# Score rows in at most two pieces, the last one negated in place with a chained minimum

## The chip, the cores and the metric

The kernel runs on one core of a Trainium2 chip. The metric is the device time of one execution in microseconds. The core has five engines with queues of their own: PE (matrix products; PEld is its weight load), DVE (VectorE), ACT (ScalarE), POOL (GpSimd) and SP, which issues the transfers. They meet only at semaphores, and each of them runs its instructions in the order in which the program lists them.

## What is computed

A decoder layer on 2048 tokens of width 1024: a normalisation, one input projection, two groups of heads, one output projection, a normalisation and the residual. The change touches differential attention alone: 8 heads, each with two score maps over 64 channels, rows of 128 queries.

```python
def diff_attention(q, k, v, lam):
    for i in range(S // Q_BLOCK):                 # 16 blocks of 128 queries
        q0 = i * Q_BLOCK
        end = q0 + Q_BLOCK
        s = jnp.einsum('bqhcd,bkhcd->bhcqk', q[:, q0:end], k[:, :end]) * scale
        ...
        p = jax.nn.softmax(jnp.where(causal, s, -jnp.inf), axis=-1)
        w = p[:, :, 0] - lam * p[:, :, 1]
        outs.append(jnp.einsum('bhqk,bkhe->bqhe', w, v[:, :end]))
```

## The kernel before

The program has five stretches: projections for the first half of the tokens (0 to about 600 us), attention of that half (to about 1090 us, called half A here), projections and the recurrence of the second half (to about 1370 us), attention of the second half (to about 2080 us, half B), and the rest of the output projection. Matrix products that have nothing to do with attention are mixed into both attention stretches as fill: projections of the second half into A (L227), the output projection into B (tile `f`, L1073).

**Units.** Attention works through units (head h, pair of query blocks pr, block t, map c). A unit is 128 rows of n x 128 score columns, n = 2 pr + t + 1. In half A n runs from 1 to 8, in half B from 9 to 16; each half has 8 heads x 16 units = 128 units. Below, "unit 14/0" is the one with n = 14 and c = 0, and "pair 14" are its two maps, 14/0 and 14/1.

**A unit's life.** Its columns are cut into pieces of SP = 512, one PSUM tile `s` each: 3 or 4 in half B. `score_mm` (L441) writes a piece with two products per 512 columns. `score_max` reduces it on DVE: all pieces but the last by a maximum into a column of `mx` (L457), the last by an addition of the causal mask that also gives the maximum (L460, with a read of the accumulator behind it); a fourth kind of instruction takes the maximum over the columns and negates it (L464, tile `nm`). `score_exp` (L480) then runs one exponential per piece on ACT, from `s` to `p`, with `nm` as bias. When both maps of a block are done, `combine` adds up the sums (L489, `lch`), makes two factors (L493, L494, `rr`) and forms p0 + factor x p1 over the whole row (L498). The result is transposed in groups of four 128x128 blocks into `pw` (L512), split into two parts by ACT (`wh`, L516) and DVE (`wl`, L517), and multiplied with the values into `o` (L535). Every second pair index a norm follows (L547 to L580).

**PSUM.** Half B has eight banks of 512 columns of f32: four tiles `s` of one bank, two `pw`, one `o`, one `f`. A piece of the next unit can be written only when the exponential of the unit that held the tile has read it. With three pieces a unit leaves one tile free; with four it leaves none.

**What sets the order.** `attention` writes, unit by unit, the exponentials of the present unit and then, by a small planner with a clock (`tp`, `free`), the next unit's score pieces between transposes, fill and value products; `combine` and the norm stand at the unit's end. The program that the tile framework makes of it lists instructions in another order where its own scheduling finds them ready at other times, so the order on each engine is read from the built program and not from the source.

Of the kernel before, what the change touches and what calls it, by code (L numbers as in the profile page):

```python
# [8 lines left out]
F32 = mybir.dt.float32  # L9
F32R = mybir.dt.float32r  # L10
BF16 = mybir.dt.bfloat16
# [17 lines left out]
MASKED = -1.0e38  # L29
SP = 512  # L30
NSA = 3
# [12 lines left out]
def hymba_kernel(  # L44
# [56 lines left out]
    make_identity(nc, ident)  # L101
    mask16 = const.tile([P, CH], BF16, name="mask16")
    nc.vector.memset(mask16, 0.0)
    ones2 = const.tile([P, 2], F32, name="ones2")
# [20 lines left out]
    def setup():  # L125
        rows, lq = su["rows"], su["lq"]
        with tc.tile_pool(name="setup", bufs=1) as sp, tc.tile_pool(name="setup_ps", bufs=1, space=PSUM) as spp:
# [4 lines left out]
            )  # L132
            nc.vector.tensor_copy(out=mask16[:, CH - P:], in_=m32)
            pt = spp.tile([P, 80], F32, name="pt")
# [255 lines left out]

    def attention(prs, kv_p, pools, nsb, per_slot, kbufs, vbufs, p1bufs):

# [34 lines left out]
        def pieces(u):  # L427
            n = (2 * u[1] + u[2] + 1) * P
            return n, [(c0, min(n, c0 + SP)) for c0 in range(0, n, SP)]

# [15 lines left out]

        def score_max(u, pi):
            n, pcs = pieces(u)
            c0, c1 = pcs[pi]
            if pi == 0:  # L450
                negm[u] = e_p.tile([P, 1], F32, tag="nm", name="nm", bufs=4)
            if pi == 0:
                sc[u, "mx"] = e_p.tile([P, 4], F32, tag="mx", name="mx", bufs=4)
            mx = sc[u, "mx"]
            s = sc[u, pi][:, 0:c1 - c0]
            if pi < len(pcs) - 1:
                nc.vector.tensor_reduce(out=mx[:, pi:pi + 1], in_=s, axis=AX.X, op=ALU.max)  # L457
                return

            nc.vector.tensor_tensor_reduce(  # L460
                out=s, in0=s, in1=mask16[:, CH - (c1 - c0):], scale=1.0, scalar=MASKED, op0=ALU.add, op1=ALU.max,
                accum_out=mx[:, pi:pi + 1],
            )
            nc.vector.tensor_reduce(out=negm[u], in_=mx[:, 0:pi + 1], axis=AX.X, op=ALU.max, negate=True)  # L464

        def score_exp(u):
# [8 lines left out]
            for pi, (c0, c1) in enumerate(pcs):  # L475
                if len(pcs) == 1:
                    acc = lch[h, pr // 2][:, (2 * pr + t) % 4, c:c + 1]
                else:
                    acc = sc[u[:3]][:, c, pi:pi + 1]
                nc.scalar.activation(  # L480
                    out=p[:, c0:c1], in_=sc.pop((u, pi))[:, 0:c1 - c0], func=AF.Exp, bias=negm[u], accum_out=acc,
                )
# [141 lines left out]
        yield  # L624
        e_p, a_p, ps_s, ps_w, ps_o, fill = pools
        for h, j in early:
            load_v(h, j)
# [4 lines left out]
        for s in range(U + 12):  # L632
# [13 lines left out]
            if u:  # L646
                score_exp(u)
            tp = 0.15 + SP / 1200.0
            free = [0.0 if k < nsb - na else tp * (k - nsb + 1 + na) + 0.1 for k in range(npc)]
# [41 lines left out]
    def attention_of(half):  # L691

        st = ExitStack()
        kv_p = st.enter_context(tc.tile_pool(name="kv" + half, bufs=2, side="right"))
        pools = []
        if half == "A":
            gen = attention(range(0, 4), kv_p, pools, NSA, lambda s: FA, 4, 4, 2)
        else:
            gen = attention(range(4, 8), kv_p, pools, 4 * CH // SP, lambda s: FB if s > 1 else 6, 6, 5, 1)
        next(gen)  # L700
        return st, pools, gen
# [333 lines left out]
    with ExitStack() as pb:  # L1035
# [3 lines left out]
        a_p = pb.enter_context(tc.tile_pool(name="attB", bufs=2, side="right"))  # L1039
        ps_s = pb.enter_context(tc.tile_pool(name="ps_sB", bufs=4 * CH // SP, space=PSUM))  # L1040
        ps_w = pb.enter_context(tc.tile_pool(name="ps_wB", bufs=2, space=PSUM))
# [156 lines left out]
```

## Time and profile before

| | |
|---|---|
| runs of the kernel | 2242.29, 2247.93, 2249.29 us, median 2247.93 |
| the profiled execution | 2245.1 us, of which the span of the trace is 2243.2 us and 1.9 us lie around it |
| PE busy | 2149.8 us (96%) |
| DVE busy | 1505.0 us (67%) |
| ACT busy | 1003.3 us (45%) |
| POOL busy | 803.1 us (36%) |
| granted PE clock over the span | 0.987 |

Matrix products are pipelined: the next one starts before the last one has ended, so a PE that is busy all the time can still be slower than its own spacing. A page's group line gives the line of the code, the engine, the tiles, the number of instructions, their busy time, the mean of one, and the idle time in front of them with what ended it.

### The profile page before, as it was taken

The numbers are of one execution on the slowest core, as the hardware profiler recorded it, in microseconds if no ns is written. First come the engines' busy times: TensorE is split into PE (matmuls) and PEld (weight loads), VectorE is DVE, ScalarE is ACT, GpSimd is POOL, SyncE is SP. The second block draws the span as 40 slices with busy tenths as digits, with TensorE's granted clock in tenths as the row PEclk, the third lists the DMA queues.
The fourth block names the chain that finished last, engine by engine and source line by source line (L and its number), as shares of the span: only waits on it lengthen the run. The fifth ranks groups of instructions, "written<-read, shape, count | busy, mean of one in ns | idle before, by whom it ended". The sixth has DMA issues, their size and how long they took to land. (4 is left out here: it accounts for less than half of the span.)

```text
span 2243.2 us, 31726 instructions
## 1 busy us (share of the span) xinstructions
PE 2149.8 (96%) x11025; PEld 1786.9 (80%) x11025; DVE 1505.0 (67%) x3296; ACT 1003.3 (45%) x2259; POOL 803.1 (36%) x741
## 2 busy tenths in 40 slices
PE   7999999999899999999999998999999999999888
PEld 7888888888688888788888776888888887888666
DVE  6531144556677767777437776888888888889775
ACT  4211133444544444444225655665656656566211
POOL 1223044434411111111265653233533335345542
PEclk9999999999999999999999998999999999999999
DMA  6554332332478666665452207455464465654573
GB/s 214 151 155 150 103 102 78 97 104 77 117 195 218 165 172 169 175 168 133 132 182 70 67 33 178 117 150 143 124 177 127 124 168 140 169 160 142 161 230 131
DMA packets 346497, 317.93 MB, mean 142 GB/s; under 512 B 20257, under 2 KB 278370, under 8 KB 346338
## 3 DMA queue, kind: packets, MB, share of 16 engines
q1 hardware_dynamic: 346338, 315.91, 50.5%
q8 instruction: 87, 1.43, 0.3%
q14 instruction: 72, 0.59, 0.1%
HBM read 221.41 MB, written 94.44 MB: 141 GB/s over the span
## 5 line engine op out<-in xcount | busy, mean ns | idle before, releaser
L227 PE MATMUL ps<-hh,whi 128*128 128x512 f32 (+1 forms) x1456 | 563.7, 387 | 0.0
L227 PE MATMUL ps<-hh,wlo 128*128 128x512 f32 (+1 forms) x1456 | 562.9, 387 | 0.0
L227 PE MATMUL ps<-hl,whi 128*128 128x512 f32 (+1 forms) x1456 | 561.5, 386 | 0.0
L480 ACT ACTIVATE p<-s,nm 128x512 f32<-128x512 f32 (+3 forms) x640 | 392.6, 623 | 325.4 <-DVE nm L464 284.3
L199 POOL TENSOR_TENSOR wlo<-wraw,whi 128x1024 fp32r<-128x1024 f32 x88 | 221.8, 2521 | 526.4 <-DVE whi L198 173.4
L441 PE MATMUL s<-ks,qs 128*128 128x512 f32 (+2 forms) x1280 | 370.5, 387 | 19.3 <-ACT p L480 15.5
L227 PEld LDWEIGHTS ps<-hl,whi 128*128 128x128 f32 x1456 | 275.3, 189 | 51.7
L457 DVE TENSOR_REDUCE mx<-s 128x1 f32<-128x512 f32 x384 | 257.8, 684 | 87.4 <-PE s L441 86.1
L227 PEld LDWEIGHTS ps<-hh,wlo 128*128 128x128 f32 x1456 | 275.2, 189 | 51.5
L227 PEld LDWEIGHTS ps<-hh,whi 128*128 128x128 f32 x1456 | 275.3, 189 | 50.5
L441 PEld LDWEIGHTS s<-ks,qs 128*128 128x128 f32 x1280 | 213.2, 191 | 76.6 <-ACT p L480 46.6
L516 ACT ACTIVATE wh<-pw 128x512 fp32r<-128x512 f32 (+1 forms) x288 | 160.3, 577 | 158.5 <-PE pw L512 155.3
L70 POOL TENSOR_SCALAR yh<-yraw 128x256 fp32r<-128x256 f32 x196 | 92.6, 491 | 354.5 <-PE f L1073 303.4
L535 PE MATMUL o<-wh,vs 128*128 128x256 f32 (+1 forms) x1152 | 217.9, 280 | 0.2 <-ACT wh L516 0.2
L535 PEld LDWEIGHTS o<-wh,vs 128*128 128x128 f32 x1152 | 192.2, 190 | 17.0 <-ACT wh L516 1.0
L517 DVE TENSOR_TENSOR wl<-pw,wh 128x512 fp32r<-128x512 f32 (+1 forms) x288 | 185.7, 654 | 29.2 <-ACT wh L516 27.4
L498 DVE SCALAR_TENSOR_TENSOR p<-p,rr,p 128x128 f32<-128x128 f32 (+15 forms) x128 | 188.3, 1471 | 3.0
L512 PE MATMUL pw<-ident,p 128*128 128x128 f32 x1088 | 171.7, 273 | 9.9 <-DVE wl L517 5.7
L1073 PE MATMUL f<-woh,yh 128*128 128x512 f32 x392 | 162.3, 414 | 12.6 <-DVE yv L1089 4.6
L512 PEld LDWEIGHTS pw<-ident,p 128*128 128x128 f32 x1088 | 133.7, 140 | 43.6 <-issue 9.4
L535 PE MATMUL o<-wl,vs 128*128 128x256 f32 x576 | 162.8, 283 | 5.2 <-DVE wl L517 4.8
L71 POOL TENSOR_TENSOR yl<-yraw,yh 128x256 fp32r<-128x256 f32 x196 | 162.6, 850 | 0.1
(165 smaller groups left out, 3278.7 us busy)
## 6 DMA issues: line engine op xcount, KB each, us to landing
wraw<-in_w_in_dram SPq DMA_DIRECT2D x96, 512.0 KB, 4.3
qs<-q_s SPq DMA_DIRECT2D x128, 256.0 KB, 4.7
ks<-k_s SPq DMA_DIRECT2D x96, 256.0 KB, 5.6
vs<-v_s SPq DMA_DIRECT2D x48, 512.0 KB, 5.6
xt<-in_x_dram SPq DMA_DIRECT2D x32, 512.0 KB, 4.4
k_s<-hilo SPq DMA_DIRECT2D x64, 256.0 KB, 3.4
q_s<-hilo SPq DMA_DIRECT2D x64, 256.0 KB, 3.4
v_s<-hilo SPq DMA_DIRECT2D x32, 512.0 KB, 4.3
```

The source lines that it names most:

```text
L71: nc.gpsimd.tensor_tensor(out=lo, in0=src, in1=hi.bitcast(F32), op=ALU.subtract)
L199: nc.gpsimd.tensor_tensor(out=lo, in0=src, in1=hi.bitcast(F32), op=ALU.subtract)
L227: nc.tensor.matmul(out=ps[:, t0:t0 + n], lhsT=a[:, k, :], rhs=b[:, k, t0:t0 + n], start=(k == 0 and m == 0), stop=(k == KC - 1 and m == 2),)
L441: nc.tensor.matmul(out=ps[:, b0 - c0:b0 - c0 + nk], lhsT=qq[:, c, t * P:(t + 1) * P], rhs=kst[h, b0 // CH][:, c, 0:nk], start=(m == 0), st ...
L457: nc.vector.tensor_reduce(out=mx[:, pi:pi + 1], in_=s, axis=AX.X, op=ALU.max)
L480: nc.scalar.activation(out=p[:, c0:c1], in_=sc.pop((u, pi))[:, 0:c1 - c0], func=AF.Exp, bias=negm[u], accum_out=acc,)
L498: nc.vector.scalar_tensor_tensor(out=p0[:, 0:n], in0=p1[:, 0:n], scalar=rr[:, 1:2], in1=p0[:, 0:n], op0=ALU.mult, op1=ALU.add,)
L512: nc.tensor.transpose(pw[:, i * P:(i + 1) * P], wts[h, pr, t][:, kb * P:(kb + 1) * P], ident)
L516: nc.scalar.activation(out=wh[:, 0:n], in_=pw[:, 0:n], func=AF.Copy)
L517: nc.vector.tensor_tensor(out=wl[:, 0:n], in0=pw[:, 0:n], in1=wh[:, 0:n].bitcast(F32), op=ALU.subtract,)
L535: nc.tensor.matmul(out=po[h, j][:, oo:oo + w1 - w0], lhsT=a[:, kb % 4, :], rhs=w[:, w0:w1], start=(kb == 0 and m == 0), stop=(kb == 2 * pr ...
L1073: nc.tensor.matmul(out=ps, lhsT=a[:, k, :], rhs=b, start=(k == 0 and m == 0), stop=(k == 7 and m == 2),)
```

## The change

Half B cuts its rows into pieces of 1024 columns (two banks) instead of 512; half A keeps 512. A unit so has at most two pieces in both halves, and half B has two tiles `s` of two banks in place of four of one bank. The first of two pieces gets its maximum, already negated, by one reduction. The last piece is negated in place as the mask is added, and its minimum begins from the first piece's result (or from a large number where there is no first), so that its accumulator is `nm` itself; the reduction over `mx` is gone. The exponential of the last piece takes the factor -1. The mask tile becomes as wide as a piece, and POOL writes it at the start of each half. The planner's estimate for a piece is 1.32 us in place of 0.58 us in half B.

```diff
-SP = 512
...
-    mask16 = const.tile([P, CH], BF16, name="mask16")
-    nc.vector.memset(mask16, 0.0)
+    mask16 = const.tile([P, P], BF16, name="mask16")
...
-    def attention(prs, kv_p, pools, nsb, per_slot, kbufs, vbufs, p1bufs):
+    def attention(prs, kv_p, pools, SP, nsb, per_slot, kbufs, vbufs, p1bufs):
...
-            if pi == 0:
-                negm[u] = e_p.tile([P, 1], F32, tag="nm", name="nm", bufs=4)
-            if pi == 0:
-                sc[u, "mx"] = e_p.tile([P, 4], F32, tag="mx", name="mx", bufs=4)
-            mx = sc[u, "mx"]
+            m = e_p.tile([P, 1], F32, tag="nm", name="nm", bufs=6)
             s = sc[u, pi][:, 0:c1 - c0]
             if pi < len(pcs) - 1:
-                nc.vector.tensor_reduce(out=mx[:, pi:pi + 1], in_=s, axis=AX.X, op=ALU.max)
-                return
-
-            nc.vector.tensor_tensor_reduce(
-                out=s, in0=s, in1=mask16[:, CH - (c1 - c0):], scale=1.0, scalar=MASKED, op0=ALU.add, op1=ALU.max,
-                accum_out=mx[:, pi:pi + 1],
-            )
-            nc.vector.tensor_reduce(out=negm[u], in_=mx[:, 0:pi + 1], axis=AX.X, op=ALU.max, negate=True)
+                nc.vector.tensor_reduce(out=m, in_=s, axis=AX.X, op=ALU.max, negate=True)
+            else:
+                nc.vector.tensor_tensor_reduce(
+                    out=s, in0=s, in1=mask[:, SP - (c1 - c0):], scale=-1.0, scalar=negm[u] if pi else -MASKED,
+                    op0=ALU.add, op1=ALU.min, accum_out=m,
+                )
+            negm[u] = m
...
-                    out=p[:, c0:c1], in_=sc.pop((u, pi))[:, 0:c1 - c0], func=AF.Exp, bias=negm[u], accum_out=acc,
+                    out=p[:, c0:c1], in_=sc.pop((u, pi))[:, 0:c1 - c0], func=AF.Exp,
+                    scale=1.0 if pi < len(pcs) - 1 else -1.0, bias=negm[u], accum_out=acc,
...
+        mask = e_p.tile([P, SP], BF16, name="mask", bufs=1)
+        nc.gpsimd.memset(mask[:, 0:SP - P], 0.0)
+        nc.gpsimd.tensor_copy(out=mask[:, SP - P:], in_=mask16)
...
-            tp = 0.15 + SP / 1200.0
+            tp = 0.15 + SP / 1200.0 if SP == CH else 0.3 + SP / 1000.0
...
-            gen = attention(range(4, 8), kv_p, pools, 4 * CH // SP, lambda s: FB if s > 1 else 6, 6, 5, 1)
+            gen = attention(range(4, 8), kv_p, pools, 2 * CH, 2, lambda s: FB if s > 1 else 6, 6, 5, 1)
...
-        ps_s = pb.enter_context(tc.tile_pool(name="ps_sB", bufs=4 * CH // SP, space=PSUM))
+        ps_s = pb.enter_context(tc.tile_pool(name="ps_sB", bufs=2, space=PSUM))
```

The built programs show what this does to the order. In the changed kernel the lines stand one to five higher: its L452 and L454 are the first piece's reduction and the last piece's minimum (with its accumulator read), L484, L488, L489 and L493 the four steps of `combine`, L512 is `wl`, L439 the scores, L507 the transposes, L1071 the fill.

DVE in half B, fourth head, pair 14, from the end of unit 13/1. The kernel before, where the row of 1664 columns that `combine` forms is that of block 13:

```order
L457 TENSOR_REDUCE mx<-s 128x1 x2
L489 TENSOR_REDUCE lch<-ls 128x2
L457 TENSOR_REDUCE mx<-s 128x1
L517 TENSOR_TENSOR wl<-pw,wh 128x512
L460 ISA s,mx<-s,mask_233 128x256
L460 ISA mx 128x1
L517 TENSOR_TENSOR wl<-pw,wh 128x512
L464 TENSOR_REDUCE nm<-mx 128x1
L493 RECIPROCAL rr<-lch 128x1
L494 SCALAR_TENSOR_TENSOR rr<-lch,neglam,rr 128x1
L498 SCALAR_TENSOR_TENSOR p_15838<-p_15909,rr,p_15838 128x1664
L457 TENSOR_REDUCE mx<-s 128x1 x2
```

The same place now:

```order
L484 TENSOR_REDUCE lch<-ls 128x2
L488 RECIPROCAL rr<-lch 128x1
L489 SCALAR_TENSOR_TENSOR rr<-lch,neglam,rr 128x1
L452 TENSOR_REDUCE nm<-s 128x1
L493 SCALAR_TENSOR_TENSOR p_15350<-p_15414,rr,p_15350 128x1664
L454 ISA s,nm<-s,mask,nm 128x768
L454 ISA nm 128x1
L512 TENSOR_TENSOR wl<-pw,wh 128x512 x2
L452 TENSOR_REDUCE nm<-s 128x1
L512 TENSOR_TENSOR wl<-pw,wh 128x384
L454 ISA s,nm<-s,mask,nm 128x768
L454 ISA nm 128x1
```

The row that `combine` forms has moved: it stood behind `nm` of unit 14/0, between two units, and now stands between that unit's maximum and its minimum.

PE in half B, fourth head, at the scores of unit 13/0. Before, `f` being the fill:

```order
L441 MATMUL s<-ks,qs 128x512 x2
L1073 MATMUL f<-wol_15136,yh 128x512
L1073 MATMUL f<-woh_15181,yh 128x512
L441 MATMUL s<-ks,qs 128x512 x4
L512 MATMUL pw<-ident,p_15297 128x128
L512 MATMUL pw<-ident,p_15431 128x128
L512 MATMUL pw<-ident,p_15297 128x128
L512 MATMUL pw<-ident,p_15431 128x128
L441 MATMUL s<-ks,qs 128x256 x2
```

The same unit's scores now:

```order
L1071 MATMUL f<-woh_14785,yl 128x512
L1071 MATMUL f<-wol_14786,yh 128x512
L439 MATMUL s<-ks,qs 128x512 x6
L439 MATMUL s<-ks,qs 128x256 x2
L1071 MATMUL f<-woh_14598,yh 128x512
```

A unit's scores stood in two or three places with other products between them; now all its products stand together, and the other work of the unit behind them.

POOL at the start of half A, where `wlo` is the split of a weight block for the fill:

```order
L327 TENSOR_TENSOR m_4565<-a 128x512
L332 TENSOR_TENSOR xc<-m_4565,xc 128x512
L197 TENSOR_TENSOR wlo<-wraw,whi 128x1024
L622 MEMSET mask 128x384
L623 COPY mask<-mask_233 128x128
L197 TENSOR_TENSOR wlo<-wraw,whi 128x1024 x2
```

The two instructions that write the mask stand behind a weight split; before, POOL did not touch the mask in this place.

More of the change, by code (lines that the diff above doesn't have):

```diff
@@ L132, in setup @@
             )
-            nc.vector.tensor_copy(out=mask16[:, CH - P:], in_=m32)
+            nc.vector.tensor_copy(out=mask16, in_=m32)
             pt = spp.tile([P, 80], F32, name="pt")
@@ L696, in attention_of @@
         if half == "A":
-            gen = attention(range(0, 4), kv_p, pools, NSA, lambda s: FA, 4, 4, 2)
+            gen = attention(range(0, 4), kv_p, pools, CH, NSA, lambda s: FA, 4, 4, 2)
         else:
-            gen = attention(range(4, 8), kv_p, pools, 4 * CH // SP, lambda s: FB if s > 1 else 6, 6, 5, 1)
+            gen = attention(range(4, 8), kv_p, pools, 2 * CH, 2, lambda s: FB if s > 1 else 6, 6, 5, 1)
         next(gen)
```

## The prediction

> **What bounds the kernel now.** I read the stretches first, one row per head of half B (its 16 units, cut at the last `nm` of each head). Columns: start and end, length, then busy time and count of PE, PEld, DVE, ACT and POOL, the granted clock, and DMA.
>
> ```profile
> 1531.97:1622.84 90.87, 87.08 (x512) 73.26 (x511) 75.51 (x174) 57.76 (x153) 39.69 (x49) 1.00 0.56 150
> 1622.84:1714.02 91.18, 88.57 (x524) 74.95 (x525) 76.39 (x174) 54.44 (x146) 36.37 (x52) 1.00 0.54 144
> 1714.02:1802.60 88.58, 86.41 (x508) 72.99 (x509) 73.26 (x173) 53.58 (x145) 28.98 (x42) 1.00 0.55 147
> 1802.60:1896.95 94.35, 90.52 (x526) 76.34 (x526) 77.99 (x174) 58.13 (x154) 46.01 (x58) 0.98 0.53 145
> 1896.95:1986.17 89.22, 87.57 (x519) 74.46 (x519) 77.17 (x178) 51.49 (x140) 27.98 (x42) 1.00 0.64 164
> ```
>
> Five heads take 90.8 us each on average. PE is idle for 1.7 to 3.8 us of a head, DVE for about 15, at full clock: PE bounds the stage, closely followed by DVE. But the busy time of pipelined products hides spacing. What they need at their own spacing comes from rows in the middle of a series:
>
> ```profile
> 1699.98 0.28 PE L535 MATMUL o<-wl,vs 128*128 128x256 f32 x1
> 1700.10 0.40 PE L535 MATMUL o<-wh,vs 128*128 128x256 f32 x2
> 1707.26 0.93 PE L512 MATMUL pw<-ident,p 128*128 128x128 f32 x7
> 1708.48 0.27 PE L512 MATMUL pw<-ident,p 128*128 128x128 f32 x1
> 607.37 0.39 PE L227 MATMUL ps<-hh,whi 128*128 128x512 f32 x1
> 607.60 0.39 PE L227 MATMUL ps<-hl,whi 128*128 128x512 f32 x1
> ```
>
> Products of 512 columns start 0.23 us apart (607.37, 607.60); two of 256 columns end 0.40 us after the first starts, one takes 0.28, so the step is 0.12; seven transposes take 0.93, one 0.27, so the step is 0.11. A head's 102 score products, 132 of fill, 156 of values, 100 transposes and 8 of the norm need 23.4 + 30.2 + 18.7 + 11.0 + 0.9, about 84 us (counted from the loops). So about 6.6 us a head are lost to waits and broken spacing. The waits of half B, with total, times and longest, say between whom:
>
> ```profile
> ACT p L480 <- DVE nm L464: 130.8, 89, 8.8
> DVE mx L457 <- PE s L441: 66.9, 64, 3.9
> PE s L441 <- ACT p L480: 11.0, 16, 1.9
> ```
>
> A circle runs through the scores. An exponential frees a PSUM tile, PE writes the next unit's piece there, DVE takes maxima, the last `nm` starts the next exponentials. One turn as the timeline has it (start, duration):
>
> ```profile
> 1597.20 0.42 DVE L460 CUSTOM_DVE_ANT_0 s<-s,mask 128x256 f32<-128x256 f32 x1
> 1597.54 0.14 DVE L460 DVE_READ_ACCUMULATOR2_ANT mx<- 128x1 f32 x1
> 1597.71 0.16 DVE L464 TENSOR_REDUCE nm<-mx 128x1 f32<-128x4 f32 x1
> 1597.96 0.69 ACT L480 ACTIVATE p<-s,nm 128x512 f32<-128x512 f32 x1 [2.75 <-DVE nm L464]
> 1598.79 0.30 PEld L441 LDWEIGHTS s<-ks,qs 128*128 128x128 f32 x2 [0.41 <-ACT p L480]
> 1598.80 0.72 PE L441 MATMUL s<-ks,qs 128*128 128x512 f32 x2
> 1599.56 1.38 DVE L457 TENSOR_REDUCE mx<-s 128x1 f32<-128x512 f32 x2 [1.69 <-PE s L441]
> 1600.85 0.15 DVE L489 TENSOR_REDUCE lch<-ls 128x2 f32<-128x8 f32 x1
> 1600.93 0.69 DVE L457 TENSOR_REDUCE mx<-s 128x1 f32<-128x512 f32 x1
> ```
>
> Unit 14/1: its masked last piece starts at 1597.20, the accumulator is read 0.08 us before its end, `nm` follows, the exponential starts at 1597.96, that is 0.34 us after the end of the masked piece. The first exponential ends at 1598.65; the weights for the next score wait 0.41 us for it and start at 1598.79, two products end at 1599.52, and DVE, idle for 1.69 us, starts at 1599.56. So from the end of an exponential to the maximum of a two-product piece: 0.91 us. DVE's next instruction starts about 0.08 us before the last one ends (1600.93 against 1601.00).
>
> **The change, part by part.** The durations (x count, then busy us and mean ns):
>
> ```profile
> L480 ACT ACTIVATE p<-s,nm 128x512 f32<-128x512 f32 x344 | 232.9, 687 | 156.4 <-DVE nm L464 130.8 <-DVE p L498 12.7 <-DVE f L563 9.8
> L480 ACT ACTIVATE p<-s,nm 128x128 f32<-128x128 f32 x32 | 11.8, 370 | 0.0
> L457 DVE TENSOR_REDUCE mx<-s 128x1 f32<-128x512 f32 x317 | 211.9, 684 | 68.0 <-PE s L441 66.9
> L460 DVE CUSTOM_DVE_ANT_0 s<-s,mask 128x512 f32<-128x512 f32 x30 | 20.6, 688 | 0.0
> L460 DVE CUSTOM_DVE_ANT_0 s<-s,mask 128x128 f32<-128x128 f32 x32 | 9.2, 289 | 3.3 <-PE s L441 3.3
> L464 DVE TENSOR_REDUCE nm<-mx 128x1 f32<-128x4 f32 x62 | 9.3, 150 | 0.6
> L517 DVE TENSOR_TENSOR wl<-pw,wh 128x512 fp32r<-128x512 f32 x163 | 109.1, 682 | 2.6 <-ACT wh L516 1.5
> L498 DVE SCALAR_TENSOR_TENSOR p<-p,rr,p 128x1664 f32<-128x1664 f32 x8 | 15.7, 1966 | 0.3
> L493 DVE RECIPROCAL rr<-lch 128x1 f32<-128x1 f32 x62 | 9.8, 158 | 0.8
> L494 DVE SCALAR_TENSOR_TENSOR rr<-lch,neglam,rr 128x1 f32<-128x1 f32 x62 | 19.8, 320 | 1.1
> ```
>
> *DVE.* From 128 to 512 columns the masked piece grows by 399 ns, 133 ns per 128; so 1024 columns take an estimated 688 + 4 x 133 = 1220 ns, for the reduction likewise (684 + 532). An n = 16 unit now takes 3 x 684 + 688 + 150 = 2890 ns (and an accumulator read in both kernels), then 2 x 1220 = 2440; n = 9 takes 2 x 684 + 289 + 148 = 1805, then 1220 + 289 = 1509. That is 0.30 to 0.45 us a unit, 6 us a head, 48 in the half. This is no path by itself: what counts is the circle.
>
> *ACT.* 370 to 687 ns over 384 columns is 106 per 128, so 1024 columns take about 1.11 us. Two exponentials in place of four save some 0.5 us at n = 16. But the first tile is freed after 1.11 us instead of 0.69, and two more products (0.46) stand in front of the first maximum: it can start 1.11 + 0.91 + 0.46 = 2.48 us after the unit's first exponential, against 1.6. That is lost. Behind the last masked piece `nm` goes: the exponential starts 0.15 us after its end instead of 0.34.
>
> *A turn now.* For the sixteen units I added up what the changed order lists on DVE from one exponential to the next, each with its duration less 0.08. Unit 14/1: 2.48, maximum 1.14, one `wl` 0.60, masked 768 columns 0.95 + 0.15: 5.3 us. Unit 14/0 has `combine` of block 13 ahead: its sums exist when both pieces are through (1.10 + 0.80 + 0.2 for the read), the reduction, the reciprocal and the factors take 0.68 more, so the maximum starts at 2.78 and ends at 3.92; now comes the combined row, 1.97 - 0.08 = 1.89, and only then the masked piece, 1.10: 6.9 us. Pair 14 so takes 12.2 us. Before, it ended at 1597.71, with pair 13 at
>
> ```profile
> 1586.45 0.16 DVE L464 TENSOR_REDUCE nm<-mx 128x1 f32<-128x4 f32 x1
> ```
>
> thus 11.3 us: this pair loses 0.9. Others win, since fewer and longer instructions stand there and `nm` is gone. By the same sums, pairs 9 to 16 take 9.7, 10.2, 11.5, 10.7, 11.9, 12.2, 10.3 and 12.6: 89.1 us a head. Their PE work, unit by unit from the changed order at the spacings above, is longer than the turn in three units, by 0.4 in all. So 89.5 against 90.8, 1.3 a head, **-10 us** in eight heads.
>
> *Bounds of this term.* The sums take no port conflicts and no drift of fill between units. One instruction added to or taken out of the turn in half the units (a `wl`, 0.6) is 0.6 x 64 = 38 us either way; PE at its own 84 us a head would be 54 us less, which I exclude as DVE waits stay. I take -10, the sum of listed rows, and keep -10 - 38 and -10 + 38 as ends.
>
> *PE order and transfers.* A unit's scores now stand together. The second piece follows 0.92 us behind the first, its exponential 1.10; the wait for weights covers most of that, a cost of at most 0.2 a unit, in the turns already. Count and size of products, q, k and v loads and all DMA issues stay; nothing is moved past SP.
>
> *Half A.* Pieces stay; `nm`'s reduction goes, 0.19 us a turn, at most 128 x 0.19 = 24 us if every unit waited for it. PE's own waits for exponentials there are
>
> ```profile
> PE s L441 <- ACT p L480: 4.5, 10, 0.7
> ```
>
> 4.5 us, so no more than that is gained, **-3 us**; the rest lies under fill. At the other end, the changed order could cost as much.
>
> *The mask.* The first masked piece of half A now needs POOL's two new instructions, and these stand behind a weight split:
>
> ```profile
> 608.63 0.29 DVE L460 CUSTOM_DVE_ANT_0 s<-s,mask 128x128 f32<-128x128 f32 x1
> 608.85 2.40 POOL L199 TENSOR_TENSOR wlo<-wraw,whi 128x1024 fp32r<-128x1024 f32 x1 [6.21 <-PE ps L227]
> 611.51 0.37 ACT L480 ACTIVATE p<-s,nm 128x128 f32<-128x128 f32 x1
> L290 POOL MEMSET xpad<- 128x4 f32 x8 | 2.7, 343 | 58.7 <-PE ps L844 41.2 <-DVE xc L298 17.5
> L199 POOL TENSOR_TENSOR gwl<-gwraw,gwh 128x256 fp32r<-128x256 f32 x8 | 6.8, 848 | 25.7 <-DVE gwh L198 25.7
> ```
>
> The masked piece started at 608.63, the split ends at 611.25. Writing 384 and copying 128 columns is not in the trace; a memset of 4 columns took 0.34, a two-operand pass of 256 took 0.85, so 0.3 to 1.7 for both, taken as 0.7. Then 0.29 for the piece and 0.24 to the exponential: 612.5 instead of 611.51, **+1 us** (0.6 to 2), as PE's next scores wait for it; behind the waiting piece stand on DVE only the masked pieces of the next units. In half B the two stand in POOL's order with over 10 us until the first maximum, and are covered by the end of the recurrence; without that cover they would cost the same 1 us.
>
> *Sum:* 2245.1 (span 2243.2 and 1.9 around it) - 10 - 3 + 1 = **2233 us**. This execution lies 2.8 us under the median of 2247.9; I hold to it.
>
> **A page's rule against it.** DVE is busy for 76 of 91 us a head and lets PE wait. The Trainium skill, "Perfetto Trace Analysis", section Optimizing Scalar/DVE Operations, says: "If Scalar/Vector aren't saturated, but are causing bubbles on other engines, breaking up instructions may allow work to be completed sooner." The change does the contrary; by that rule rival (2) below would win. The trace agrees in part: with short pieces DVE starts 1.6 us into a turn, not 2.48.
>
> **The rivals.** (1) *PE hides it* (0.25). Pairs 9 and 10 have PE work close to 10 us by the order; if these and 12 stay at what they were, gains and losses in the others cancel, only half A moves: 2243. For it: PE is 96% busy. Against: 6.6 us a head are not products. (2) *The combined row in the turn* (0.25). In pairs 11 to 14 it now stands between maximum and minimum, while no spare PSUM tile lets PE go ahead. Pairs 13 and 14 lose 0.6 and 0.9 against the 11.3 of before; if the gain in 9 to 12 does not come, because a three-piece unit had a free tile and now has none, this is 1.5 x 8 = 12 us more: 2245 + 12 - 2 = 2255. It decides from the point where the sixteen turns together take longer than the 90.8 of before. For it: four pairs read that way in the order. Against: PE has fill behind each group of scores. (3) *DVE was the real limit* (0.05): all 6 us a head come through, 2245 - 48 = 2197.
>
> **Numbers.** The forecast has 0.45. About 0.3% (7 us) is what a measurement of this kernel can tell from no change. Below 2238 lie (3) and the forecast but for 0.02 at its upper edge: faster 0.45 + 0.05 - 0.02 = 0.48. Those 0.02 and (1), less 0.01 for its own upper edge: same 0.26. (2) and that 0.01: slower 0.26. The range takes in rival 2 and most of the B term's ends (2233 - 28 and 2233 + 38, rounded) and leaves out rival 3: 2205 to 2270.
>
> **What would show it.** Half B: a head of 89 to 90 us, unit 14/0 near 6.9 and 14/1 near 5.3, DVE busy 70 us a head; exponentials of 1024 columns at 1.11 and reductions at 1.22 us. Rival 1 shows the same turns but heads at 90.8 with PE idle below 2 us; rival 2 PE idle above 5 us a head on exponentials. Half A: first exponential 1 us later against the score products, PE's waits below 4.5. I would be wrong if long instructions over two banks cost more than the slope says, or if the combined row fell elsewhere in time than the order suggests.

## The result, and the profile after

The changed kernel takes 2273.53 us (median of 4 runs, 2269.76 to 2279.27) against 2245.47 for the kernel before on the same chip: a ratio of 1.0126, 95% interval 1.0097 to 1.0156. It is 1.3% slower, where 0.5% faster was forecast. Its profiled execution took 2279.27 us, the longest of the four, and the span is 2277.2 (before: 2243.2). So the traces lie 34 us apart and the medians 28.

The five heads of half B that the prediction began with now read (same columns, each head cut where its last unit's exponentials begin):

```profile
1556.84:1650.34 93.50, 87.52 (x506) 71.87 (x506) 72.58 (x132) 52.33 (x107) 39.50 (x50) 1.00 0.58 149
1650.34:1743.44 93.10, 86.89 (x506) 71.79 (x506) 72.64 (x132) 47.94 (x99) 28.77 (x42) 1.00 0.54 128
1743.44:1835.01 91.57, 87.21 (x509) 72.31 (x509) 72.58 (x132) 48.28 (x98) 28.42 (x42) 1.00 0.54 129
1835.01:1929.62 94.61, 89.77 (x518) 74.53 (x518) 74.96 (x134) 52.14 (x106) 42.59 (x58) 1.00 0.57 158
1929.62:2019.07 89.45, 86.12 (x501) 72.23 (x501) 74.01 (x137) 45.43 (x94) 30.22 (x42) 1.00 0.55 145
```

92.4 us a head on average, against 90.8 before and 89.5 forecast. DVE did become lighter (73 us a head instead of 76) and ACT too, but PE now stands idle for 3.3 to 6.2 us of a head. The durations came out as worked out, but for one (x count, busy us, mean ns; the last two rows are of half A):

```profile
L474 ACT ACTIVATE p<-s,nm 128x1024 f32<-128x1024 f32 x143 | 159.2, 1115 | 154.6 <-DVE nm L454 137.1 <-DVE rr L488 4.6 <-DVE f L79 4.5
L452 DVE TENSOR_REDUCE nm<-s 128x1 f32<-128x1024 f32 x128 | 156.2, 1221 | 60.9 <-PE s L439 58.6
L454 DVE CUSTOM_DVE_ANT_0 s<-s,mask,nm 128x1024 f32<-128x1024 f32 x16 | 20.5, 1283 | 0.0
...
L454 DVE CUSTOM_DVE_ANT_0 s<-s,mask,nm 128x384 f32<-128x384 f32 x16 | 9.9, 622 | 3.0 <-PE s L439 2.6
L454 DVE CUSTOM_DVE_ANT_0 s<-s,mask 128x384 f32<-128x384 f32 x16 | 9.0, 560 | 7.7 <-PE s L439 7.7
```

1115 and 1221 ns stand for 1.11 and 1.22 us. The minimum that begins from `nm` takes 62 ns more than the same instruction with a constant (622 against 560), so 1283 instead of the 1220 worked out.

Who waits for whom in half B, before (rows beside those that the prediction shows) and after:

```profile
PEld s L441 <- ACT p L480: 32.8, 75, 2.4
DVE lch L489 <- ACT p L480: 15.1, 12, 1.7
...
DVE wl L517 <- ACT wh L516: 1.5, 5, 0.5
...
PEld o L535 <- ACT wh L516: 0.4, 1, 0.4
...
PEld pw L512 <- DVE wl L517: 0.2, 1, 0.2
```

```profile
DVE lch L484 <- ACT p L474: 75.7, 54, 3.9
...
PEld s L439 <- ACT p L474: 43.1, 61, 3.4
...
PE s L439 <- ACT p L474: 24.1, 27, 3.1
...
DVE wl L512 <- ACT wh L511: 17.8, 36, 2.2
...
PEld pw L507 <- DVE wl L512: 8.3, 23, 1.0
...
PEld o L530 <- ACT wh L511: 7.3, 21, 0.5
```

Three things grew: `lch`, the first step of `combine`, holds DVE's queue while it waits for exponentials (15.1 to 75.7 us), PE waits longer for exponentials ahead of scores (11.0 to 24.1, its weight load 32.8 to 43.1), and the parts `wh` and `wl` come late for DVE, the transposes and the values, where these rows had next to no wait before.

**A ledger for PE.** PE has the same 11025 products in every kernel here. I took, from product to product, the distance of their starts less the step of an undisturbed series (0.229 us for 512 columns, 0.174 for 384, 0.118 for 256, 0.110 for a transpose), and call the sum PE's loss. With the same products, span less loss has to come out the same (2100.3 to 2100.8 us in the table). So the ledger proves nothing by its sum; what it does is to split the difference of two spans by stretch. It does not move when products only change place, as a head's length does: head 1 of the changed kernel is 15.6 us longer, but has 12.6 us more of products in it. The stretches are bounded about where exponentials start, those of a half's first unit or of a head's last, and a wait across a bound is booked where it begins.

| kernel | ahead of A | half A | between | B head 1 | B heads 2-7 | B head 8 | after | sum |
|---|---|---|---|---|---|---|---|---|
| before | 20.6 | 20.8 | 17.2 | 13.5 | 34.8 | 6.7 | 29.2 | 142.8 |
| changed | 22.2 | 16.3 | 23.2 | 15.9 | 56.8 | 17.3 | 24.9 | 176.6 |
| e1 half A only | 21.8 | 13.3 | 21.0 | 10.7 | 34.9 | 10.1 | 29.8 | 141.6 |
| e10 e1, combine late | 21.3 | 16.4 | 21.9 | 10.6 | 30.8 | 8.9 | 28.9 | 138.8 |
| e5 e1, lch early | 22.3 | 16.9 | 21.6 | 12.0 | 50.6 | 14.1 | 24.2 | 161.7 |
| e3 changed, combine late | 22.2 | 16.7 | 22.2 | 17.3 | 45.2 | 21.1 | 27.5 | 172.2 |
| e2 changed, old maxima | 23.6 | 14.7 | 23.6 | 15.8 | 65.3 | 16.7 | 29.8 | 189.5 |

The 33.8 us between the first two rows are +1.6, -4.5 and +6.0 up to half B, +35.0 in half B (22.0 of it in heads 2 to 7, 10.6 in head 8), and -4.3 behind it. The rows are one execution each. Half A is the same code in all of them but the first, and its loss goes from 13.3 to 16.9, so a difference of less than about 4 us in a stretch says nothing. Of the 10.6 in head 8, 3.2 are a wait that begins at its very end; booked behind it they would turn the -4.3 into -1.1.

### The profile page after: what moved, and what is told of

The parts are those of the page before. It is cut to its first block, busy times and chain, and to the rows that moved or that the text cites. A ratio compares the mean times of both kernels' runs of the same rounds, so it can differ in the third digit from the quotient of the medians.

```text
span 2277.2 us, 30895 instructions
## 1 busy us (share of the span) xinstructions
PE 2164.0 (95%) x11025; PEld 1792.7 (79%) x11025; DVE 1477.9 (65%) x2847; ACT 957.4 (42%) x1875; POOL 792.2 (35%) x745
## 5 line engine op out<-in xcount | busy, mean ns | idle before, releaser
L474 ACT ACTIVATE p<-s,nm 128x1024 f32<-128x1024 f32 (+2 forms) x448 | 345.7, 777 | 318.1 <-DVE nm L454 269.6
L439 PE MATMUL s<-ks,qs 128*128 128x512 f32 (+2 forms) x1280 | 332.9, 383 | 31.6 <-ACT p L474 29.5
L439 PEld LDWEIGHTS s<-ks,qs 128*128 128x128 f32 x1280 | 222.8, 190 | 96.5 <-ACT p L474 57.2
L452 DVE TENSOR_REDUCE nm<-s 128x1 f32<-128x1024 f32 (+1 forms) x192 | 200.1, 1042 | 82.0 <-PE s L439 79.7
L530 PE MATMUL o<-wh,vs 128*128 128x256 f32 (+1 forms) x1152 | 226.1, 286 | 0.3 <-ACT wh L511 0.3
L512 DVE TENSOR_TENSOR wl<-pw,wh 128x512 fp32r<-128x512 f32 (+1 forms) x288 | 187.2, 656 | 44.5 <-ACT wh L511 43.9
L530 PEld LDWEIGHTS o<-wh,vs 128*128 128x128 f32 x1152 | 187.6, 191 | 17.3 <-ACT wh L511 7.8
L507 PE MATMUL pw<-ident,p 128*128 128x128 f32 x1088 | 175.6, 276 | 13.5 <-DVE wl L512 4.3
L493 DVE SCALAR_TENSOR_TENSOR p<-p,rr,p 128x128 f32<-128x128 f32 (+15 forms) x128 | 182.6, 1426 | 1.9
L1071 PE MATMUL f<-woh,yh 128*128 128x512 f32 x392 | 162.1, 414 | 19.0 <-ACT fo L1097 10.6
L507 PEld LDWEIGHTS pw<-ident,p 128*128 128x128 f32 x1088 | 132.7, 142 | 50.2 <-DVE wl L512 8.3
L530 PE MATMUL o<-wl,vs 128*128 128x256 f32 x576 | 168.9, 293 | 3.3 <-DVE wl L512 3.2
L1071 PE MATMUL f<-wol,yh 128*128 128x512 f32 x392 | 161.9, 413 | 0.0
```

The source lines that it names most:

```text
L439: nc.tensor.matmul(out=ps[:, b0 - c0:b0 - c0 + nk], lhsT=qq[:, c, t * P:(t + 1) * P], rhs=kst[h, b0 // CH][:, c, 0:nk], start=(m == 0), st ...
L452: nc.vector.tensor_reduce(out=m, in_=s, axis=AX.X, op=ALU.max, negate=True)
L474: nc.scalar.activation(out=p[:, c0:c1], in_=sc.pop((u, pi))[:, 0:c1 - c0], func=AF.Exp, scale=1.0 if pi < len(pcs) - 1 else -1.0, bias=neg ...
L493: nc.vector.scalar_tensor_tensor(out=p0[:, 0:n], in0=p1[:, 0:n], scalar=rr[:, 1:2], in1=p0[:, 0:n], op0=ALU.mult, op1=ALU.add,)
L507: nc.tensor.transpose(pw[:, i * P:(i + 1) * P], wts[h, pr, t][:, kb * P:(kb + 1) * P], ident)
L512: nc.vector.tensor_tensor(out=wl[:, 0:n], in0=pw[:, 0:n], in1=wh[:, 0:n].bitcast(F32), op=ALU.subtract,)
```

## The experiments

Theory T1: the order of `combine` on DVE is the loss. T2: pieces of 1024 in two tiles are. T3: the minimum that starts from `nm`, a value read from a tile (called its pointer below) in place of a constant, is.

**e1_half_a.** Half B as before, half A as changed (`attention` of B with pieces `CH` and four tiles, the old branch of `score_max` for `prs[0] > 0`).

> Half A of the changed kernel (two pieces at most, the last one negated, chained minimum, mask written by POOL), with half B of the kernel before (pieces of 512, four tiles, maxima gathered in mx and reduced to nm). All theories put the loss into half B, where the changed kernel takes 744 us from first to last unit against 708, so half B should take 708 within 4 here. Half A should begin 2 us later than before and take 457 us to its last unit against 462.5. Theory A1: the 5.8 us that the stretch between the halves gains in the changed kernel is due to half B's own start (its mask and its first, coarse unit): then the gain of half A stays and the time is 2239 to 2243 us. Theory A2: PE has a fixed amount of products to do by then, and what half A saves comes back behind it: the time is that of the kernel before, 2244 to 2248 us.

Measured: 2243.69 us, ratio 0.9986 (0.9974 to 0.9997). Half B is that of before (708.8 us from first to last unit). PE's loss falls by 7.5 us in half A and rises by 3.8 behind it, 2.0 of that in one wait of the gate product of the recurrence and 2.2 in one of `f`. The time lies between the ranges of A1 and A2, and what came back speaks for A2. All of the loss is in half B.

**e2_coarse_only**, the counterpart in half B: coarse pieces with the old reductions.

> As the changed kernel, but half B reduces as the kernel before does: maximum of the first 1024 into mx, mask added to the last piece with a maximum, and a third reduction to nm. Pieces of 1024 and the two tiles of two banks stay. Theory T2 (two coarse tiles without a spare are the loss): the loss stays, and the reduction to nm, about 0.1 us of work on DVE with what stands around it in each of 128 units, comes on top: 2275 to 2290 us. Theory T1 (the loss comes from where the combine steps stand on DVE, between two units' maxima): here the combined row stands between a unit's maximum and its nm 15 times in half B, against 22 times between maximum and minimum in the changed kernel, but its first step still stands ahead of the next unit's first maximum 64 times of 64: 2268 to 2280 us. Theory T3 (the minimum that begins from a pointer is 65 ns slower): 2265 us.

Measured: 2291.62 us, 1.0192 (1.0175 to 1.0209), above the numbers of T1 and, by a little, of T2. With pieces of 1024 the chained minimum so saves 15 us by the ratios, 18 by the medians; neither it nor its pointer (T3) is what makes the changed kernel slower than before.

**e3_combine_late.**

```diff
-        def combine(h, pr, t):
+        def combine(h, pr, t, after=None):
...
+                if prs[0] > 0 and after in negm:
+                    nc.vector.tensor_copy(out=l2[:, 0:1], in_=negm[after])
                 nc.vector.tensor_reduce(
...
-            run("C", combine)
+            run("C", lambda *a: combine(*a, u))
```

> The changed kernel with one addition: in half B a copy of one column ties the first step of combine (lch) to nm of the next block's first unit, so that lch, the two factors and the combined row all stand behind that unit's minimum and ahead of the maximum of its second map. Nothing else is changed; 64 copies are added. Theory T1 (DVE's queue is held by lch, which waits 75.7 us for exponentials in half B against 15.1 before, and by rows that stand between a maximum and its minimum): nearly all of lch's wait goes, and the time falls by 15 to 25 us, to 2248 to 2258 us. Theory T2 (no spare tile, coarse pieces): PE waits for the exponentials as it did, and the time stays within 6 us of the changed kernel, 2267 to 2280 us. A third result, slower than the changed kernel, would mean that the row in front of the second map's maximum costs more than the place it had.

Measured: 2270.61 us, 1.0109 (1.0091 to 1.0127). DVE's wait at `lch` is gone (idle time in the last columns):

```profile
L486 DVE TENSOR_REDUCE lch<-ls 128x2 f32<-128x4 f32 x63 | 9.8, 156 | 1.6
```

but only 3 us of time came back, and the intervals of the two ratios overlap. T1 as the main cause falls. In heads 2 to 7 the loss fell by 11.6; head 8 took 3.8 back, by one long wait, which ACT's timeline shows:

```profile
2034.81 0.63 ACT L975 ACTIVATE woh<-woraw 128x512 fp32r<-128x512 f32 x1 [6.21 <-DMA woraw<-in_w_out_dram]
2038.97 0.63 ACT L975 ACTIVATE woh<-woraw 128x512 fp32r<-128x512 f32 x1 [3.53 <-DMA woraw<-in_w_out_dram]
2040.01 0.63 ACT L975 ACTIVATE woh<-woraw 128x512 fp32r<-128x512 f32 x1 [0.41 <-DMA woraw<-in_w_out_dram]
2040.55 1.10 ACT L474 ACTIVATE p<-s,nm 128x1024 f32<-128x1024 f32 x1
```

The roundings of the next set of output weights stand ahead of a unit's exponentials in ACT's queue and wait for transfers; PE lost 9.05 us ahead of the scores behind them. The changed kernel has the same wait in head 8 with 2.97 us, and PE lost 3.3 there.

**e4_chain_512**, pieces of 512 with the chained minimum: the columns of `mx` are reduced ahead of the last piece.

> Half A of the changed kernel; half B with pieces of 512 in four tiles as before, but negated and chained: the maxima of all pieces but the last go to mx, their reduction gives the negated maximum while the last piece is still being multiplied, and the last piece's minimum begins from it and gives nm. So the small reduction leaves the path from the last piece to the exponentials, at the price of 65 ns for the pointer. Theories T1 and T2 both expect a gain over the kernel before: some 0.2 us for each of 112 units outside pairs where PE is the limit, at most half of it kept since PE loses only 6.6 us a head: 2232 to 2242 us. Theory T3 (the pointer's minimum decides): 2248 to 2256 us.

Measured: 2250.62 us, 1.0013 (1.0002 to 1.0025), 7 us above e1. T1 and T2 both missed; the time is in T3's range. The same count of instructions stands on DVE for a unit, and the last one is longer by its pointer: 62 ns in 128 units are 8 us if each of them counted, which no run shows.

**e5_lch_early.** T1's cost put into fine pieces, on top of e1.

```diff
+                if pi == 0 and "last" in sc:
+                    nc.vector.tensor_scalar(
+                        out=mx, in0=ident[:, 0:4], scalar1=sc.pop("last")[:, 0:1], scalar2=None, op0=ALU.mult,
+                    )
...
             if u:
                 score_exp(u)
+                if prs[0] > 0 and u[3]:
+                    sums(*u[:3])
```

`sums` is `combine`'s first step, taken out of it, and leaves its result in `sc["last"]`.

> The kernel of e1_half_a, so half B in pieces of 512 with four tiles, and in it the first step of combine (lch) is issued right behind the exponentials and tied to the next block's maxima: a product of four columns with it fills mx first. So lch stands ahead of the next block's first maximum for all blocks, as it does in the changed kernel, where e1_half_a has it there 25 to 39 times of 64. 64 small products on DVE are added, each in a turn. Theory T1 (order of combine): of the 22 us that PE loses more in heads 2 to 7 of the changed kernel, tying combine late took back 11.6; made early with fine pieces it should cost as much, 2250 to 2262 us, with lch's wait for the exponentials near 60 us instead of 17. Theory T2 (coarse pieces): 64 x 0.15 us at most, 2244 to 2250 us.

Measured: 2267.61 us, 1.0093 (1.0077 to 1.0108); `lch` waits 78.2 us, as in the changed kernel. So this order costs 24 us with fine pieces, its 64 added products of four columns included (0.23 us each, 15 us if all of them counted; T2 had allowed 10 for them), and T1's number was even too low. One turn shows how (start, duration):

```profile
1705.96 0.69 ACT L492 ACTIVATE p<-s,nm 128x512 f32<-128x512 f32 x1 [1.89 <-DVE nm L466]
...
1706.91 0.62 PE L439 MATMUL s<-ks,qs 128*128 128x512 f32 x2
...
1707.96 0.48 ACT L492 ACTIVATE p<-s,nm 128x256 f32<-128x256 f32 x1
...
1708.56 0.16 DVE L500 TENSOR_REDUCE lch<-ls 128x2 f32<-128x8 f32 x1 [2.10 <-ACT p L492]
1708.76 0.23 DVE L456 TENSOR_SCALAR mx<-ident,lch 128x4 f32<-128x4 f32 x1
...
1709.42 1.88 DVE L460 TENSOR_REDUCE mx<-s 128x1 f32<-128x512 f32 x3
```

The next unit's first piece is written at 1707.53, but DVE stands before `lch` until the last of four exponentials is through; the maxima begin at 1709.42. Now the same place with coarse pieces, in the changed kernel:

```profile
1720.26 1.12 ACT L474 ACTIVATE p<-s,nm 128x1024 f32<-128x1024 f32 x1 [3.07 <-DVE nm L454]
...
1721.52 1.69 PEld L439 LDWEIGHTS s<-ks,qs 128*128 128x128 f32 x8 [0.60 <-ACT p L474]
1721.52 2.02 PE L439 MATMUL s<-ks,qs 128*128 128x512 f32 x8 [0.17 <-ACT p L474]
...
1722.38 0.16 DVE L484 TENSOR_REDUCE lch<-ls 128x2 f32<-128x4 f32 x1 [2.21 <-ACT p L474]
...
1722.76 1.23 DVE L452 TENSOR_REDUCE nm<-s 128x1 f32<-128x1024 f32 x1
...
1725.38 1.11 ACT L474 ACTIVATE p<-s,nm 128x1024 f32<-128x1024 f32 x1 [2.54 <-DVE nm L454]
...
1726.63 1.20 PE L439 MATMUL s<-ks,qs 128*128 128x512 f32 x4 [1.01 <-ACT p L474]
```

`lch` waits 2.21 us here too, but by the prediction's own sum the first reduction starts 2.48 us after the exponentials anyway, at 1722.74, and it does at 1722.76. In this turn the wait is long and free, because the coarse piece itself is that late. And ahead of 1726.63 PE stands for 1.01 us, since a score is next in its queue: no tile is free until a whole exponential of 1.11 us is through. If other turns are like these two, which I didn't follow one by one, that is why taking the wait away (e3) gives so little and putting it in (e5) costs so much.

**e6_const_mask**: e1 with the mask of before (`mask = mask16`).

> The kernel of e1_half_a with the mask kept as before the change: one tile of 512 columns, filled by DVE at the program's start, so that no unit waits for POOL at the start of half A. Half A began 1.8 to 2.2 us later with POOL's mask. Theory: the first exponential comes 2 us earlier and PE's loss ahead of half A falls from 21.8 to 20.6 us: 2240 to 2243 us. Rival: PE is busy with projections there, and the time stays within 1 us of e1_half_a, 2243 to 2245 us.

Measured: 2245.26 us, 0.9987 (0.9973 to 1.0000). Half A began 4.1 us earlier than in e1, PE's loss ahead of it fell from 21.8 to 18.5, and the time did not follow: the rival.

**e7_late_weights_early**: e3 with the transfers of `woraw` at `k == 0` instead of `k == 3`.

> The kernel of e3_combine_late, and the first four transfers of the next set of output weights (woraw) are issued at the first step of the group ahead of the change of sets instead of its fourth. In e3_combine_late ACT waited 9.7 us for such a transfer in the eighth head, and PE once lost 9.05 us ahead of a score product. Theory: that stall goes or shrinks to 3 us or less, and the time is 2261 to 2265 us; what then stays over the kernel before is 15 to 19 us. Rival: the stall has another place or cause, and the time stays at 2268 to 2274 us.

Measured: 2273.65 us, 1.0121 (1.0103 to 1.0138); the stall stayed, with 9.79 us. Moving four transfers ahead misses it, so the rival's "another cause" holds: there are four `woraw` tiles, and the transfers waited for are issued only when POOL's `wol` has read the ones ahead (from 2026.50 to 2031.37 us), and they land from 2033.66 to 2040.56, so much of the wait is the transfers themselves.

**e8_planner_07**: the changed kernel with 0.7 in place of 0.3 + SP / 1000.

> The changed kernel with one number of the planner changed: 0.7 us for a piece of half B instead of 1.32, so that score products are put ahead of fill, transposes and value products where they now stand behind them (some 200 of PE's instructions change place). Theory T2 as a matter of placement (PE stands before a tile that isn't free): PE waits longer ahead of scores, 30.6 us in heads 2 to 7 becomes 36 or more, and the time rises by 3 to 12 us, to 2276 to 2286 us. Rival: the turn is what limits, the earlier scores shorten it, and the time falls to 2262 to 2270 us.

Measured: 2277.76 us, 1.0134 (1.0113 to 1.0154), in the theory's range, but also within noise of the changed kernel. The loss ahead of scores in heads 2 to 7 stayed (30.8 against 30.6): neither mechanism showed, and the planner's number is not the cause.

**e9_combine_later**: e3 with `nx` in place of `u`.

> As e3_combine_late, but the copy takes nm of the next block's second map, so that the steps of combine stand one unit later: behind that unit's minimum and ahead of the first maximum of the block after it. In e3_combine_late the turns into the second map of a block were longer than in the changed kernel (49.1 us a head against 45.1) and those into the first shorter (42.5 against 47.3). Theory R (what e3 left over the kernel before, 10 us in heads 2 to 7, is the row of 1152 to 2048 columns that stands ahead of the second map's maximum): the turns into the second map go back to 45 us a head, those into the first grow, and the time is 2268 to 2276 us, as e3 within its noise, since the row then stands ahead of another maximum. Theory T2 (coarse pieces cost 10 us in heads 2 to 7 wherever the row stands): PE's loss in heads 2 to 7 is 42 to 50 us and the wait ahead of scores stays above 28 us. If the loss fell to 38 us or less, T2 would be wrong.

Measured: 2444.11 us, 1.087 (1.0846 to 1.0895). Neither theory saw that coming:

```profile
ACT p L474 <- DVE p L495: 184.5, 48, 7.0
PE pw L509 <- DVE p L495: 65.8, 38, 4.7
```

Half B keeps one tile for the second map's exponentials (its last argument, `p1bufs`, is 1), and the combined row frees it. Behind the next second map's minimum, the row stands in front of those exponentials. It is no measure of T2.

**e10_half_a_late**: e1 with the copy of e3.

> The kernel of e1_half_a with the copy of e3_combine_late in half B, so fine pieces and combine behind the next block's first nm. In e1_half_a lch waits 17 us for exponentials and stands ahead of the next block's first maximum 25 to 39 times of 64. Theory T1: with fine pieces, where the order is good already, little is left to take: PE's loss in heads 2 to 7 stays at 33 to 36 us and the time is 2240 to 2247 us. Rival: the row ahead of the second map's maximum costs as much as lch's order did: 2250 to 2260 us, and then e3 would owe part of its time to that place.

Measured: 2240.17 us, 0.9958 (0.9944 to 0.9973). The copy costs nothing with fine pieces, and may gain: the ratio's interval just clears that of e1. The 4.1 us less of loss in heads 2 to 7 are no more than the ledger's noise. This is the fastest kernel of the study, faster than both.

**e11_chain_late**: e4 with the copy of e3.

> The kernel of e4_chain_512 with the same copy. Its rows and lch stood behind nm or between two maxima in most blocks. Candidate for a version better than both: the reduction to nm is off the path and combine is out of it. Theory T1: 2238 to 2248 us. Rival: in fine pieces PE sets the time whatever is taken from the turn, since e4 shortened the turns of pairs 9 and 10 by 2.6 us a head and PE's loss in heads 2 to 7 stayed at 36.6 us: 2247 to 2254 us.

Measured: 2258.38 us, 1.0040 (1.0023 to 1.0057), 18 us above e10 and slower than e4: the loss in heads 2 to 7 is 42.9 and in head 8 17.0, with a stall of 3.5 and one of 3.7 us where ACT waits for weights. Both theories missed. The chained minimum does not pay with pieces of 512 in either order. The two stalls are 7 of the 18 us; the other 11 I didn't settle.

**e12, e13, e14.** e3, e10 and the changed kernel, with `woh` made by POOL (`nc.gpsimd.tensor_scalar`, twice a factor of 1.0).

> e3_combine_late, and the rounded half of each output weight tile (woh) is made by POOL, as it makes yh, instead of ACT, so that no transfer of weights stands ahead of an exponential in ACT's queue. In e3_combine_late ACT waited 15.3 us for woraw in half B and PE lost 9.05 us in one place of head 8. Theory: that stall goes, PE's loss in half B falls from 83.6 to 70 to 76 us, and the time is 2258 to 2264 us; what stays over e10_half_a_late (2240), some 18 to 24 us, is then the price of pieces of 1024 in two tiles. Rival: with the stall gone, coarse pieces cost less than 8 us: 2240 to 2248 us. Third: POOL, with about 46 us of rounding more, becomes late with yh and wol, and the time stays at 2268 us or above.

> e10_half_a_late with woh made by POOL, as in e12. ACT waited only 3.1 us for woraw there, so little is to be had: 2236 to 2242 us. If POOL's added work matters by itself, 2243 us or more, and e12 has to be read with that difference taken off.

> The changed kernel with woh made by POOL, as in e12. ACT waited 7.2 us for woraw in half B and PE lost 3.3 us at one such place in head 8. Theory: 3 to 5 us come back, 2268 to 2271 us, and the order of combine, the difference to e12, is worth 6 to 13 us with coarse pieces. Rival: the weights are behind more of the loss than their waits show: 2262 us or less.

Measured, on one chip: 2269.20 us (1.0089, 1.0068 to 1.0109), 2246.64 (0.9991, 0.9978 to 1.0004) and 2280.46 (1.0139, 1.0116 to 1.0161). By their times none came out as its first theory: e12 is in its third outcome, e13 in its second, 6 us above e10, and in e14 nothing came back. POOL's added work seems to cost something by itself, but the trace of e13, its fastest of 12 executions (2239.39), doesn't show where. So the kernels are compared within the three. Combine late instead of as in the changed kernel is worth 11.3 us with coarse pieces (2280.46 less 2269.20). Half B with coarse pieces and their chain instead of fine ones with the old maxima costs 22.6 us with `combine` late (2269.20 less 2246.64). This price is in the 18 to 24 of e12's theory, and its rival falls. PE still lost 4.0 and 5.0 us in two places, now behind transfers of `ks` and of `yv`, the norm's input. No run has coarse pieces with the old maxima and `combine` late, so the chain's part of the 22.6 is not known.

What coarse pieces do to PE is read where `combine` is late in both, e3 first, then e10:

```profile
PEld s L439 <- ACT p L474: 56.5, 86, 9.1
...
PE s L439 <- ACT p L474: 31.9, 29, 8.9
```

```profile
PEld s L439 <- ACT p L488: 34.5, 79, 2.4
PE s L439 <- ACT p L488: 11.2, 18, 1.9
```

PE's loss ahead of scores alone is 31.2 against 22.3 us in heads 2 to 7, 12.6 against 7.7 in head 1.

The ledger also says which products come late. PE's loss in heads 2 to 7, ahead of scores / ahead of all its other products (transposes, values, fill and the norm's), in us:

| | `combine` late | `lch` ahead of the next maxima |
|---|---|---|
| fine pieces | e10: 22.3 / 8.5 | e5: 26.7 / 23.9 |
| coarse pieces | e3: 31.2 / 14.0 | changed: 30.6 / 26.2 |

The early `lch` adds 12 to 15 us ahead of the other products, and 4 us or nothing ahead of scores. Coarse pieces add 4 to 9 us ahead of scores.

## Why the prediction was wrong

**What bounds it** was right: PE, through the circle of scores, maxima and exponentials. The durations of the rows above were right but for the pointer's 62 ns.

**A turn now** is where it failed, in the sum "89.5 against 90.8, 1.3 a head, -10 us in eight heads". The single turns were near: unit 14/1 took 5.4 us (5.3 worked out), 14/0 6.3 (6.9). By pairs 9 to 16 the five heads took 9.7, 10.5, 12.9, 11.9, 12.5, 11.7, 10.4 and 12.9, against 9.7, 10.2, 11.5, 10.7, 11.9, 12.2, 10.3 and 12.6: the sum was mis-sized by 3 us a head, nearly all of it in pairs 11 to 13. (Before, the same pairs took 11.7, 9.0, 10.4, 12.4, 11.5, 11.0, 11.8 and 13.0: pair 9 did win, pair 11 lost 2.4.) A turn was taken as the sum of DVE's list, with PE's other work under it. But PE waits in its own order: for tiles, and also for `wl`, `wh` and the combined row (10.4 us ahead of transposes, 2.4 before), which come late when DVE's queue stands: with `combine` late (e3) the loss ahead of products other than scores is 12 us smaller. In heads 2 to 7 its loss ahead of scores grew by 6.1 us, ahead of transposes and values by 11.6, and ahead of fill by 3.9. What made pair 11 so much longer than its sum (1.4 us) stays open.

The second half of the same step failed too: five heads were taken for eight, and their length for time. Fill had moved from them into head 1, so the five hold 2.1 us a head less of products than before; their length grew by 1.6 us a head, the loss in heads 2 to 7 by 3.7. Head 8 lost 10.6 us more, 9.2 of it in three places: 3.3 where ACT waits for weights, 2.7 and 3.2 where transposes wait for steps of a norm on DVE.

**The forecast's -10 had the wrong sign, +35 in half B.** Rival 2 had the mechanism, no tile free ahead of a coarse unit and the combined row in the turn, and the sign, but its 2255 was too small by 18 us, since it priced pairs 13 and 14 alone, and not a PE that stands before tiles, transposes and values all along the head. The experiments split its two halves: they don't add. Fine pieces with `combine` late 2240, fine with `lch` early 2268 (its 64 added products of four columns among it), coarse with `combine` late 2271, coarse as changed 2274 (on different chips, where the kernel before took 2245 to 2250). Either is enough for most of the loss, though 9 us of e3's are the wait behind weights. In the changed kernel itself the coarse pieces with their chain are the larger part, and the order is worth 3 to 11 us. The rival's sign, PE idle above 5 us a head, was seen in two heads of five (3.3 to 6.2), and only part of it is ahead of exponentials. The rule of the Trainium skill that the prediction set against itself (Perfetto Trace Analysis, Optimizing Scalar/DVE Operations) held here: DVE at 73 of 92 us a head was not saturated, and with longer instructions PE waited longer ahead of scores (31.2 us against 22.3).

**Rivals 1 and 3** fell: rival 1 wanted heads of 90.8 us with PE idle below 2, and they took 92.4 with 3.3 to 6.2; rival 3 wanted DVE's savings as time, and DVE saved 3 us a head while the heads grew.

**Half A, -3**: right as a net figure, partly by luck: PE's loss there fell by 4.5, in e1 by 7.5, more than the bound of 4.5 allowed, and 3.8 (e1) to 6.0 us came back in the stretch behind, which the sum left out. e1's ratio makes the whole of it 3 us.

**The mask, +1**: the masked piece started at 611.99, worked out 612.0; the first exponential at 613.71, worked out 612.5. Before and after:

```profile
610.21 1.28 ACT L480 ACT_TABLE_LOAD   x1
611.51 0.37 ACT L480 ACTIVATE p<-s,nm 128x128 f32<-128x128 f32 x1
```

```profile
611.66 0.29 POOL L623 COPY mask<-mask 128x128 bf16<-128x128 bf16 x1
611.99 0.30 DVE L454 CUSTOM_DVE_ANT_0 s<-s,mask 128x128 f32<-128x128 f32 x1 [3.15 <-POOL mask L623]
...
612.41 1.28 ACT L474 ACT_TABLE_LOAD   x1 [2.09 <-DVE nm L454]
613.71 0.37 ACT L474 ACTIVATE p<-s,nm 128x128 f32<-128x128 f32 x1
```

The term left out the table load in front of the first exponential, which here waits with it for `nm`. It is 2.2 us late, and e6 shows that the time hardly notices.

## What to carry to other kernels

Fewer, longer instructions on an engine that isn't the bound lower its busy time and lengthen the hand-off: ask when the first result is handed on and whether the bound engine has other work until then. A wait in an in-order queue is worth what stands ready behind it, not its length: 76 us of waiting cost 3 to 11 us where the next input was late anyway, and 78 us cost some 24, with the small products that made them, where it wasn't. Keep a ledger of the bound engine's lost spacing by stretch; lengths of stretches move when work only changes place.

## What the runs showed of the hardware that was not expected

- DVE's masked minimum takes 57 to 62 ns more when its starting value is a pointer (622 against 560 ns at 384 columns, 753 against 696 at 512).
- The activation table's load takes 1.28 us, and it can wait for the input of the exponential behind it: ahead of half A's first exponential it started only when `nm` was there (612.41 us). It doesn't always: ahead of half B's it ran at 1366.70, 9.9 us before the exponential. What decides is open. The Trainium skill, ScalarE: Activation LUTs, section What ACT_TABLE_LOAD costs, gives about 1283 ns for it, as here, and 1380 ns more for a drain; here the exponential starts 1.30 us after the load does, so no drain shows behind it, and before the change it started 0.02 us after ACT's last instruction ended, so none shows ahead of it.
